# Short convolution and spatial gating: transposes off TensorE, tap products on ScalarE

## The chip, the cores and the metric

The kernel runs on one core of a Trainium2 chip (trn2). The metric is the time of one execution in device microseconds (us); each kernel is run several times and the median is given. The profile is taken from one execution of its own, whose span runs from the first to the last instruction of the core.

## The reference

A trunk of four layers works on x, 256 tokens by 1024 channels, in float32. Each layer is

```
x = x + 0.5 * swiglu(rms_norm(x), gate, up, down)      # D_FF = 2816
x = x + mixer(rms_norm(x))
x = x + 0.5 * swiglu(rms_norm(x), gate, up, down)
```

and the mixer is the short gated convolution in layers 0 and 3, latent attention in layer 1, and the spatial-gating MLP in layer 2. The two that matter here:

```
def short_conv_mixer(x, w_in, conv_k, w_out):
    b, c, h = split(x @ w_in, 3)               # 1024 channels each
    z = c * h
    conv[t] = k[0]*z[t-2] + k[1]*z[t-1] + k[2]*z[t]     # per channel, causal
    return (b * conv) @ w_out

def spatial_gating_mixer(x, w_in, v_norm, w_s, b_s, w_out):
    u, v = split(gelu(x @ w_in), 2)
    mixed = causal w_s over chunks of 128 tokens of rms_norm(v) + b_s
    return (u * mixed) @ w_out
```

## The kernel before, in words

**Tiles and products.** The tokens are two tiles of 128, each worked on by a stream of its own (stream 0 and stream 1, a Python generator each). Every product x @ w is done in split float32: weights and activations are each cut into a high part (fp32r) and a low part, and `products` (L293 to L302) issues three matmuls per 128 rows of weights and 512 columns: high by high (L299), high by low (L300), low by high (L302). The activations are the stationary operand, so they have to stand with channels on the partitions. The weights come in units of 128 x 1024 values: SyncE loads `raw` (L93), ScalarE makes `whi` (L106), VectorE makes `wlo` (L113). Six raw buffers and nine buffers for made units; a unit is made four units ahead of stream 0 (`AHEAD`).

**Order.** Nothing is reordered by a scheduler: the order of the program is the order on each engine's queue, and each queue is worked off in order. `advance(t)` lets one stream go on to its next yield, which is as a rule one unit: six matmuls of 512 columns. One such advance is called a turn here. Stream 0 gets four turns ahead, then the streams alternate, stream 1 first; so stream 1 does the same step seven turns after stream 0. Weights are made in stream 0's turns.

**Work that is put off.** `later(n, fn)` puts a piece of work off by a number of turns; `run_due` issues what is due at the end of each turn, in order of due turn and then of registration. The counter is raised between the stream's step and `run_due`, so a piece put off by n from a stream's step in turn a is issued at the end of turn a+n-1; put off from another put-off piece, at the end of the n-th turn after it.

**The convolution block** of a stream, in steps of one unit each: before the change the steps 1 to 12 are a group of three products, c0, h0 and b0 (halves of 512 columns; done at steps 8, 10, 12), then c1 (13 to 16), h1 (17 to 20), b1 (21 to 24). Steps 25 to 32 are the product with w_out in `rows_into_x`: steps 25 to 28 take channels of half 0 (`ms[0]`), 29 and 30 those of half 1 (`ms[1]`) for output columns 0 to 511, 31 and 32 for columns 512 to 1023. `c_done` copies its bank to SBUF on ScalarE (L544), `h_done` multiplies on VectorE (L548) to z, `b_done` copies on ScalarE (L553). `convolved` turns z with four PE transposes (L261 in `transposed`), copies them on ScalarE to zT (L523, 128 x 512), and makes the convolution on VectorE: four 128 x 128 products (L528) and eight multiply-adds (L530). `gated` turns b with four PE transposes, multiplies on VectorE (L537), and `split` makes the high part on ScalarE (L253) and the low part on VectorE (L254).

**Two ways to turn.** x itself is turned at the block ends either by PE (`turn_by_pe`) or, in `prepare_x`, by a 32 x 32 block transpose on VectorE (L415), a write of 256 KB to DRAM (L421) and four reads of 64 KB (L425) on SyncE's queue, and four 128 x 128 activations on ScalarE that scale while they copy (L431, `take`, 12 turns after). Weight loads are held back (`W.hold`) from the write until the reads are issued. `turned` does the same for the feed-forward's hidden values.

**The spatial block.** `u_mixed` (L639) multiplies, `gated` turns with PE and splits (`lhs_of`), for both halves, two turns later.

Of the kernel before, what the change touches and what calls it, by code (L numbers as in the profile page):

```python
# [48 lines left out]
CHAIN_AHEAD = 3  # L49
LAG = 4  # L50
DOWN_TAIL, OUT_TAIL = 12, 4
X_TURN, X_WRITE, X_READ, X_TAKE = 2, 1, 3, 12
IDLE_FIRST, IDLE_DMA, IDLE_PE, IDLE_MLA = 1, 2, 2, 4
SKEW = 2
K_POOL, K_SUM, K_SCALE, K_TURN, Q_ROPE, Q_TURN, Q_SUM, Q_WAIT = 2, 2, 3, 2, 1, 3, 3, 3
# [76 lines left out]
def trunk(ctx: ExitStack, tc: tile.TileContext, x, positions, norm_g, ffn_gate, ffn_up, ffn_down,  # L132
# [76 lines left out]
    def column(at, n=1):  # L209
        return columns[1][:, at : at + n]  # L210
# [39 lines left out]
    def split(src, shape):  # L250

        hi, lo = slot(shape, F32R), slot(shape, F32R)
        nc.scalar.activation(hi, src, AF.Copy)  # L253
        nc.vector.tensor_tensor(out=lo, in0=src, in1=hi.bitcast(F32), op=ALU.subtract)  # L254
        return hi, lo

    def transposed(parts):

        tr = trp()
        for n, part in enumerate(parts):  # L260
            nc.tensor.transpose(tr[: part.shape[-1], n, :], part, ident)  # L261
        return tr
# [129 lines left out]
    def x_half(t, h):  # L392
        return xs[t][:, h * 512 : (h + 1) * 512]
# [12 lines left out]
    def prepare_x(t, h, i, which, halves_by_dma):  # L406

        g = gain_at(i, which, h)
        lhs[t][h] = None
        later(1, lambda: square_x(t, h))  # L410
        if not halves_by_dma[h]:
            later(X_TURN, lambda: turn_by_pe(t, h, g))
            return
        z = slot([P, 4, 4, 32])
        nc.vector.transpose(z.rearrange("p j k b -> p k j b"), x_half(t, h).rearrange("p (k j b) -> p k j b", j=4, b=32))  # L415
        d = dram.tile([4, 32, 4, 4, 32], F32, tag="xturn", name=name("xturn"))
        y = slot([P, 4, 4, 32])

        def write():
            W.hold(1)  # L420
            nc.sync.dma_start(out=d.rearrange("i a j k b -> (i a) j k b"), in_=z)  # L421

        def read():
            for j in range(4):
                nc.sync.dma_start(out=y[32 * j : 32 * j + 32], in_=d[:, :, j].rearrange("i a k b -> a i k b"))  # L425
            W.hold(-1)

        def take():
            xg = slot([P, 4, P])
            for k in range(4):  # L430
                nc.scalar.activation(xg[:, k, :].rearrange("p (i b) -> p i b", b=32), y[:, :, k], AF.Copy, scale=g[:, k : k + 1])  # L431
            lhs[t][h] = split(xg, [P, 4, P])

        later(X_WRITE, write)
        later(X_READ, read)
        later(X_TAKE, take)

    def turn_by_pe(t, h, g):
        tr = transposed([xs[t][:, (4 * h + k) * P : (4 * h + k + 1) * P] for k in range(4)])
# [64 lines left out]


    def plan_conv(ia):
        plan_group([(conv_w_in[ia], part * D) for part in (1, 2, 0)], 512, NK)
        for part in (1, 2, 0):
            W.add(conv_w_in[ia], part * D + 512, 512, NK, 2)
        plan_rows(conv_w_out[ia], NK, OUT_TAIL)  # L510

    def conv(t, i, ia, shared, then):
        a, r = yield from normed(t, IDLE_DMA)
        ms = [None] * 2

        def convolved(j, z):
            zp = transposed([z[:, k * P : (k + 1) * P] for k in range(4)])
            zT = slot([P, 4, P + 2])
            if t == 0:
                nc.vector.memset(zT[:, :, 0:2], 0.0)  # L520
            else:
                nc.vector.tensor_copy(out=zT[:, :, 0:2], in_=shared["z", t - 1, j][:, :, P : P + 2])
            nc.scalar.activation(zT[:, :, 2 : P + 2], zp, AF.Copy)  # L523
            shared["z", t, j] = zT
            cv = slot([P, 4, P])
            for k in range(4):
                taps = [column(C_CONV + (3 * ia + w) * NK + 4 * j + k) for w in range(3)]
                nc.vector.tensor_scalar(cv[:, k, :], zT[:, k, 0:P], taps[0], None, op0=ALU.mult)  # L528
                for w in (1, 2):
                    nc.vector.scalar_tensor_tensor(out=cv[:, k, :], in0=zT[:, k, w : w + P], scalar=taps[w],  # L530
                                                   in1=cv[:, k, :], op0=ALU.mult, op1=ALU.add)
            shared["cv", t, j] = cv

        def gated(j, bs):
            bT = transposed([bs[:, k * P : (k + 1) * P] for k in range(4)])
            m = slot([P, 4, P])
            nc.vector.tensor_tensor(out=m, in0=bT, in1=shared["cv", t, j], op=ALU.mult)  # L537
            ms[j] = split(m, [P, 4, P])

        cs = [None] * 2  # L540

        def c_done(j, ps):
            cs[j] = slot([P, 512])
            nc.scalar.activation(cs[j], ps, AF.Copy, scale=r)  # L544

        def h_done(j, ps):
            z = slot([P, 512])
            nc.vector.scalar_tensor_tensor(out=z, in0=ps, scalar=r, in1=cs[j], op0=ALU.mult, op1=ALU.mult)  # L548
            later(3, lambda: convolved(j, z))

        def b_done(j, ps):
            bs = slot([P, 512])
            nc.scalar.activation(bs, ps, AF.Copy, scale=r)  # L553
            later(2, lambda: gated(j, bs))

        yield from linear_group(t, a, 512, NK, [lambda ps, f=f: f(0, ps) for f in (c_done, h_done, b_done)])
        for f in (c_done, h_done, b_done):
            f(1, (yield from linear(t, a, 512, NK)))
            yield
        yield from rows_into_x(t, lambda k: ms[k // 4], NK, OUT_TAIL, 1.0, then)  # L560

# [31 lines left out]
    def spatial(t, i, ic, _, then):  # L593
# [30 lines left out]
                                    in1=column(C_SGB + 4 * j, 4).unsqueeze(2).broadcast_to([P, 4, P]))  # L624
            mixed[j] = mx

        def gated(j, m):
            ms[j] = lhs_of(m, 4)

        us = [None] * 2  # L630

# [5 lines left out]
        def u_mixed(j):  # L637
            m = slot([P, 512])
            nc.vector.tensor_tensor(out=m, in0=us[j], in1=mixed[j].rearrange("p k n -> p (k n)"), op=ALU.mult)  # L639
            later(2, lambda: gated(j, m))  # L640

        yield from linear_group(t, a, 512, NK, [v_done, v_done, lambda ps: u_done(0, ps)])
        u_done(1, (yield from linear(t, a, 512, NK)))
# [392 lines left out]
```

## Time and profile before

| | |
|---|---|
| median of 3 runs | 1859.11 us (1858.88 to 1860.58) |
| the profiled execution | 1856.6 us |
| its span | 1854.9 us, mean granted TensorE clock 0.998 |
| PE busy | 1833.3 us, 99% of the span |
| VectorE (DVE) busy | 1119.6 us, 60% |
| ScalarE (ACT) busy | 913.9 us, 49% |
| GpSimd (POOL) busy | 103.9 us, 6% |
| DMA | mean 216 GB/s, 400.26 MB |

Busy time is the time in which an engine had at least one instruction in work; waits and instruction issue don't count. On PE the instructions overlap, so the distance from one start to the next tells what one costs. In a timeline a row is one or more like instructions in a row; the bracket tells how long the engine stood idle before it and what released it. The clock of 1 means 2.4 GHz, 0.5 means 1.2 GHz.

### The profile page before, as it was taken

How to read it: one execution, taken by the hardware profiler on the slowest of the kernel's cores; microseconds unless marked ns; L12 is line 12 of the kernel's file. 1: busy time of each engine (PE TensorE's matmuls, PEld its weight loads, DVE VectorE, ACT ScalarE, POOL GpSimd, SP SyncE). 2: the span in 40 equal slices, each digit the busy share in tenths (PEclk: the TensorE clock that was granted, in tenths of full speed). 3: DMA queues.
4: the chain of work that ended last, by engine and by line, in shares of the span. 5: the costliest groups of instructions: out<-in, count | busy, mean ns of one | idle time of the engine just before them, and what ended most of it. 6: DMA issues, size and time to landing. Idle time of an engine off the chain costs nothing.

```text
span 1854.9 us, 23375 instructions
## 1 busy us (share of the span) xinstructions
PE 1833.3 (99%) x8518; PEld 1506.0 (81%) x8518; DVE 1119.6 (60%) x1357; ACT 913.9 (49%) x1300; POOL 103.9 (6%) x222
## 2 busy tenths in 40 slices
PE   8999999999999989999999999999999999999999
PEld 6888878888888878888888888888888888788887
DVE  5655676655665576666556555665645665775662
ACT  5443645443644376544454446554545454545451
POOL 1000000000501031000010001000000000000000
PEclk9999999999999999999999999999999999999999
DMA  7776657776777550687777766577857785657782
GB/s 265 241 240 218 209 179 216 240 241 210 235 244 238 193 160 15 201 259 232 221 238 256 228 220 216 175 232 234 264 185 243 242 261 178 213 181 235 233 269 75
DMA packets 228980, 400.26 MB, mean 216 GB/s; under 512 B 17126, under 2 KB 77696, under 8 KB 228864
## 3 DMA queue, kind: packets, MB, share of 16 engines
q1 hardware_dynamic: 227856, 397.08, 67.0%
q8 instruction: 66, 1.08, 0.2%
q0 software_dynamic: 608, 1.11, 0.2%
q10 hardware_dynamic: 400, 0.57, 0.1%
q14 instruction: 50, 0.41, 0.1%
HBM read 365.67 MB, written 33.03 MB: 215 GB/s over the span
## 4 chain that ended last, share of the span: by engine, by line
PE 96%; ACT 2%; DVE 2%; issue 0%; DMA 0%; DVEq 0%; ACTq 0%
PE acc L299 31%; PE acc L300 31%; PE acc L302 31%; PE tr L261 1%; PE acc L938 1%; PE acc L911 1%; ACT whi L106 1%; DVE wlo L113 0%; DVE s L530 0%; ACT s L836 0%; ACT s L253 0%; PE acc L620 0%; DMA s<-in_norm_g_dram 0%; ACT s L817 0%; ACT s L860 0%
## 5 line engine op out<-in xcount | busy, mean ns | idle before, releaser
L299 PE MATMUL acc<-whi,s 128*128 128x512 f32 (+1 forms) x2664 | 1025.2, 385 | 2.8 <-ACT whi L106 1.3
L300 PE MATMUL acc<-wlo,s 128*128 128x512 f32 (+1 forms) x2664 | 1019.8, 383 | 2.1 <-DVE wlo L113 2.1
L302 PE MATMUL acc<-whi,s 128*128 128x512 f32 (+1 forms) x2664 | 988.2, 383 | 0.0
L113 DVE TENSOR_TENSOR wlo<-raw,whi 128x1024 fp32r<-128x1024 f32 (+1 forms) x634 | 747.3, 1212 | 131.0 <-ACT whi L106 129.2
L106 ACT ACTIVATE whi<-raw 128x1024 fp32r<-128x1024 f32 (+1 forms) x634 | 636.6, 1047 | 138.9 <-PE acc L302 120.3
L299 PEld LDWEIGHTS acc<-whi,s 128*128 128x128 f32 x2664 | 500.9, 188 | 107.8 <-ACT whi L106 2.5
L300 PEld LDWEIGHTS acc<-wlo,s 128*128 128x128 f32 x2664 | 501.0, 188 | 106.0 <-DVE wlo L113 3.0
L302 PEld LDWEIGHTS acc<-whi,s 128*128 128x128 f32 x2664 | 500.7, 188 | 106.1 <-DVE s L254 0.7
L479 ACT ACTIVATE s<-acc,rstd 128x512 f32<-128x512 f32 (+1 forms) x96 | 62.6, 652 | 446.4 <-PE acc L302 440.4
L487 DVE SCALAR_TENSOR_TENSOR s<-acc,rstd,s 128x512 f32<-128x512 f32 (+1 forms) x96 | 67.7, 705 | 173.6 <-PE acc L302 171.8
L286 DVE TENSOR_TENSOR s<-big,s 128x512 fp32r<-128x512 f32 x96 | 61.8, 644 | 128.1 <-ACT s L285 127.9
L381 ACT ACTIVATE s<-x 128x512 bf16<-128x512 f32 x48 | 30.2, 630 | 163.6 <-DVE x L400 125.9
L254 DVE TENSOR_TENSOR s<-s,s 128x512 fp32r<-128x512 f32 (+1 forms) x58 | 39.9, 688 | 107.6 <-ACT s L253 107.6
L389 POOL TENSOR_TENSOR total<-ss,ss 128x1 f32<-128x1 f32 x26 | 14.8, 570 | 1417.1 <-ACT s L381 1417.1
L400 DVE SCALAR_TENSOR_TENSOR x<-acc,x 128x512 f32<-128x512 f32 x32 | 22.1, 692 | 117.3 <-PE acc L302 117.2
L285 ACT ACTIVATE s<-big 128x512 fp32r<-128x512 f32 x96 | 56.3, 586 | 22.1 <-DMA big<-turn 22.0
L489 DVE STREAM_TRANSPOSE big<-s 128x512 f32<-128x512 f32 (+1 forms) x96 | 64.1, 667 | 3.3
L253 ACT ACTIVATE s<-s 128x512 fp32r<-128x512 f32 (+1 forms) x58 | 36.5, 629 | 42.1 <-DVE s L537 21.6
L431 ACT ACTIVATE s<-s,columns 128x128 f32<-128x128 f32 x136 | 43.1, 388 | 1.9 <-DMA s<-xturn 1.7
L261 PE MATMUL tr<-ident,s 128*128 128x128 f32 (+1 forms) x222 | 33.3, 276 | 9.8 <-DVE s L781 5.1
L261 PEld LDWEIGHTS tr<-ident,s 128*128 128x128 f32 (+1 forms) x222 | 25.8, 138 | 17.9 <-DVE s L781 7.3
L415 DVE STREAM_TRANSPOSE s<-x 128x512 f32<-128x512 f32 x34 | 24.2, 711 | 1.2
(123 smaller groups left out, 410.6 us busy)
## 6 DMA issues: line engine op xcount, KB each, us to landing
raw<-in_ffn_gate_dram SPq DMA_DIRECT2D x176, 512.0 KB, 4.8
raw<-in_ffn_up_dram SPq DMA_DIRECT2D x176, 512.0 KB, 5.0
raw<-in_ffn_down_dram SPq DMA_DIRECT2D x176, 512.0 KB, 5.0
raw<-in_conv_w_in_dram SPq DMA_DIRECT2D x48, 512.0 KB, 4.7
turn<-big SPq DMA_DIRECT2D x32, 512.0 KB, 4.0
big<-turn SPq DMA_DIRECT2D x128, 128.0 KB, 4.4
xturn<-s SPq DMA_DIRECT2D x34, 256.0 KB, 4.2
s<-xturn SPq DMA_DIRECT2D x136, 64.0 KB, 2.0
```

The lines of the kernel that those rows point to most:

```text
L106: nc.scalar.activation(hi, src, AF.Copy)
L113: self.nc.vector.tensor_tensor(out=lo, in0=src, in1=hi.bitcast(F32), op=ALU.subtract)
L261: nc.tensor.transpose(tr[: part.shape[-1], n, :], part, ident)
L285: nc.scalar.activation(hi.rearrange("p k (i b) -> p k i b", b=32), src, AF.Copy)
L286: nc.vector.tensor_tensor(out=lo.rearrange("p k (i b) -> p k i b", b=32), in0=src, in1=hi.bitcast(F32).rearrange("p k (i b) -> p k i b", b ...
L299: nc.tensor.matmul(ps, lhsT=ah[:, k, :], rhs=wh[:, wk, c], start=first, stop=False)
L300: nc.tensor.matmul(ps, lhsT=ah[:, k, :], rhs=wl[:, wk, c], start=False, stop=False)
L302: nc.tensor.matmul(ps, lhsT=al[:, k, :], rhs=wh[:, wk, c], start=False, stop=last)
L431: nc.scalar.activation(xg[:, k, :].rearrange("p (i b) -> p i b", b=32), y[:, :, k], AF.Copy, scale=g[:, k : k + 1])
L479: nc.scalar.activation(sg[n], ps[:, :w], AF.Silu, scale=r)
L487: nc.vector.scalar_tensor_tensor(out=h, in0=ps[:, :w], scalar=r, in1=sg[n], op0=ALU.mult, op1=ALU.mult)
L489: nc.vector.transpose(z[0][:, :, k0 : k0 + w // P].rearrange("p j k b -> p k j b"), h.rearrange("p (k j b) -> p k j b", j=4, b=32))
```

## The change

z and b in the convolution, and the second half of the gate in the spatial block, are turned in the way that x is: VectorE block transpose, DMA to DRAM and back. The function `turn_half` is cut out of `prepare_x` for it. The tap products go from VectorE to ScalarE: four copies of 128 x 128 into zT, twelve activations of 128 x 128 with the tap as scale, one tile per tap; VectorE adds the three tiles one turn later. The two columns ahead of zT are filled by GpSimd. The products of the block are done in another order: the group is c0, h0, c1 (done at steps 8, 10, 12), then h1 (16), b0 (20), b1 (24). `Z_TAKE` and `M_TAKE` are both 9.

```diff
-X_TURN, X_WRITE, X_READ, X_TAKE = 2, 1, 3, 12
+X_TURN, X_WRITE, X_READ, X_TAKE, Z_TAKE, M_TAKE = 2, 1, 3, 12, 9, 9
...
+    def turn_half(src, take, turns):
+
         z = slot([P, 4, 4, 32])
-        nc.vector.transpose(z.rearrange("p j k b -> p k j b"), x_half(t, h).rearrange("p (k j b) -> p k j b", j=4, b=32))
-        d = dram.tile([4, 32, 4, 4, 32], F32, tag="xturn", name=name("xturn"))
+        nc.vector.transpose(z.rearrange("p j k b -> p k j b"), src.rearrange("p (k j b) -> p k j b", j=4, b=32))
+        d = dram.tile([4, 32, 4, 4, 32], F32, tag="xturn", name=name("xturn"), bufs=8)
         y = slot([P, 4, 4, 32])
 
         def write():
...
         later(X_WRITE, write)
         later(X_READ, read)
-        later(X_TAKE, take)
+        later(turns, lambda: take(y))
...
-        plan_group([(conv_w_in[ia], part * D) for part in (1, 2, 0)], 512, NK)
-        for part in (1, 2, 0):
-            W.add(conv_w_in[ia], part * D + 512, 512, NK, 2)
+        w = conv_w_in[ia]
+        plan_group([(w, D), (w, 2 * D), (w, D + 512)], 512, NK)
+        for c in (2 * D + 512, 0, 512):
+            W.add(w, c, 512, NK, 2)
...
-        def convolved(j, z):
-            zp = transposed([z[:, k * P : (k + 1) * P] for k in range(4)])
+        def convolved(j, y):
             zT = slot([P, 4, P + 2])
             if t == 0:
-                nc.vector.memset(zT[:, :, 0:2], 0.0)
+                nc.gpsimd.memset(zT[:, :, 0:2], 0.0)
             else:
-                nc.vector.tensor_copy(out=zT[:, :, 0:2], in_=shared["z", t - 1, j][:, :, P : P + 2])
-            nc.scalar.activation(zT[:, :, 2 : P + 2], zp, AF.Copy)
+                nc.gpsimd.tensor_copy(out=zT[:, :, 0:2], in_=shared["z", t - 1, j][:, :, P : P + 2])
+            for k in range(4):
+                nc.scalar.activation(zT[:, k, 2 : P + 2].rearrange("p (i b) -> p i b", b=32), y[:, :, k], AF.Copy)
             shared["z", t, j] = zT
-            cv = slot([P, 4, P])
-            for k in range(4):
-                taps = [column(C_CONV + (3 * ia + w) * NK + 4 * j + k) for w in range(3)]
-                nc.vector.tensor_scalar(cv[:, k, :], zT[:, k, 0:P], taps[0], None, op0=ALU.mult)
-                for w in (1, 2):
-                    nc.vector.scalar_tensor_tensor(out=cv[:, k, :], in0=zT[:, k, w : w + P], scalar=taps[w],
-                                                   in1=cv[:, k, :], op0=ALU.mult, op1=ALU.add)
+            cv = [slot([P, 4, P]) for _ in range(3)]
+            for w in range(3):
+                for k in range(4):
+                    nc.scalar.activation(cv[w][:, k, :], zT[:, k, w : w + P], AF.Copy, scale=column(C_CONV + (3 * ia + w) * NK + 4 * j + k))
+            later(1, lambda: summed(j, cv))
+
+        def summed(j, parts):
+            cv = parts[0]
+            for part in parts[1:]:
+                nc.vector.tensor_tensor(out=cv, in0=cv, in1=part, op=ALU.add)
             shared["cv", t, j] = cv
 
-        def gated(j, bs):
-            bT = transposed([bs[:, k * P : (k + 1) * P] for k in range(4)])
+        def gated(j, y):
             m = slot([P, 4, P])
-            nc.vector.tensor_tensor(out=m, in0=bT, in1=shared["cv", t, j], op=ALU.mult)
+            nc.vector.tensor_tensor(out=m.rearrange("p k (i b) -> p i k b", b=32), in0=y,
+                                    in1=shared["cv", t, j].rearrange("p k (i b) -> p i k b", b=32), op=ALU.mult)
             ms[j] = split(m, [P, 4, P])
...
-            later(3, lambda: convolved(j, z))
+            turn_half(z, lambda y: convolved(j, y), Z_TAKE)
...
-            later(2, lambda: gated(j, bs))
-
-        yield from linear_group(t, a, 512, NK, [lambda ps, f=f: f(0, ps) for f in (c_done, h_done, b_done)])
-        for f in (c_done, h_done, b_done):
-            f(1, (yield from linear(t, a, 512, NK)))
+            turn_half(bs, lambda y: gated(j, y), M_TAKE)
+
+        yield from linear_group(t, a, 512, NK, [lambda ps: c_done(0, ps), lambda ps: h_done(0, ps), lambda ps: c_done(1, ps)])
+        for f, j in ((h_done, 1), (b_done, 0), (b_done, 1)):
+            f(j, (yield from linear(t, a, 512, NK)))
             yield
...
-        def gated(j, m):
-            ms[j] = lhs_of(m, 4)
+        def gated(j, y):
+            src = y.rearrange("p i k b -> p k i b")
+            hi, lo = slot([P, 4, P], F32R), slot([P, 4, P], F32R)
+            nc.scalar.activation(hi.rearrange("p k (i b) -> p k i b", b=32), src, AF.Copy)
+            nc.vector.tensor_tensor(out=lo.rearrange("p k (i b) -> p k i b", b=32), in0=src,
+                                    in1=hi.bitcast(F32).rearrange("p k (i b) -> p k i b", b=32), op=ALU.subtract)
+            ms[j] = hi, lo
...
-            later(2, lambda: gated(j, m))
+            if j == 0:
+                later(2, lambda: gated_by_pe(j, m))
+            else:
+                turn_half(m, lambda y: gated(j, y), M_TAKE)
```

## Rows read from the trace of the kernel before

**Rows 1.** Page, busy time of each engine, share of the span, instructions.

```profile
PE 1833.3 (99%) x8518; PEld 1506.0 (81%) x8518; DVE 1119.6 (60%) x1357; ACT 913.9 (49%) x1300; POOL 103.9 (6%) x222
```

**Rows 2.** Page, the chain that ended last, by engine and by line.

```profile
PE 96%; ACT 2%; DVE 2%; issue 0%; DMA 0%; DVEq 0%; ACTq 0%
```

**Rows 3.** Timeline, PE: one turn of six matmuls; start us, duration us.

```profile
204.64 0.39 PE L302 MATMUL acc<-whi,s 128*128 128x512 f32 x1
...
206.03 0.39 PE L302 MATMUL acc<-whi,s 128*128 128x512 f32 x1
```

**Rows 4.** Timeline, first convolution, stream 0: h0 done, then its transposes.

```profile
218.60 0.39 PE L302 MATMUL acc<-whi,s 128*128 128x512 f32 x1
218.83 0.39 PE L299 MATMUL acc<-whi,s 128*128 128x512 f32 x1
...
219.11 0.75 DVE L548 SCALAR_TENSOR_TENSOR s<-acc,rstd,s 128x512 f32<-128x512 f32 x1
...
221.38 0.39 PE L302 MATMUL acc<-whi,s 128*128 128x512 f32 x1
221.61 0.60 PE L261 MATMUL tr<-ident,s 128*128 128x128 f32 x4
221.97 0.48 PE L299 MATMUL acc<-whi,s 128*128 128x512 f32 x1
...
222.28 0.40 PE L300 MATMUL acc<-wlo,s 128*128 128x512 f32 x1
```

**Rows 5.** Timeline, PE, second convolution, stream 1: transposes that came late.

```profile
1607.76 0.40 PE L302 MATMUL acc<-whi,s 128*128 128x512 f32 x1
1609.09 0.66 PE L261 MATMUL tr<-ident,s 128*128 128x128 f32 x4 [0.93 <-DVE s L548]
```

**Rows 6.** Timeline, ScalarE: a bank copied, then the next instruction.

```profile
223.22 0.39 PE L302 MATMUL acc<-whi,s 128*128 128x512 f32 x1
...
223.45 0.40 PE L299 MATMUL acc<-whi,s 128*128 128x512 f32 x1
...
223.71 0.69 ACT L544 ACTIVATE s<-acc,rstd 128x512 f32<-128x512 f32 x1 [0.86 <-PE acc L302]
...
224.29 1.05 ACT L106 ACTIVATE whi<-raw 128x1024 fp32r<-128x1024 f32 x1
```

**Rows 7.** Timeline, ScalarE: four scaled copies, and three weight units.

```profile
187.46 1.26 ACT L431 ACTIVATE s<-s,columns 128x128 f32<-128x128 f32 x4
...
215.91 2.94 ACT L106 ACTIVATE whi<-raw 128x1024 fp32r<-128x1024 f32 x3
```

**Rows 8.** Groups by line and form: count, busy us, mean ns, idle before.

```profile
L113 DVE TENSOR_TENSOR wlo<-raw,whi 128x1024 fp32r<-128x1024 f32 x626 | 739.7, 1215 | 129.5 <-ACT whi L106 128.6 <-DMA raw<-in_ffn_up_dram 0.5 <-DMA turn<-big 0.3
L431 ACT ACTIVATE s<-s,columns 128x128 f32<-128x128 f32 x136 | 43.1, 388 | 1.9 <-DMA s<-xturn 1.7
L254 DVE TENSOR_TENSOR s<-s,s 128x512 fp32r<-128x512 f32 x56 | 38.8, 693 | 106.4 <-ACT s L253 106.4
L253 ACT ACTIVATE s<-s 128x512 fp32r<-128x512 f32 x56 | 35.4, 632 | 38.6 <-DVE s L537 21.6 <-DVE s L441 15.9
L415 DVE STREAM_TRANSPOSE s<-x 128x512 f32<-128x512 f32 x34 | 24.2, 711 | 1.2
L530 DVE SCALAR_TENSOR_TENSOR s<-s,columns,s 128x128 f32<-128x128 f32 x64 | 22.5, 352 | 2.3
L398 DVE TENSOR_TENSOR x<-acc,x 128x512 f32<-128x512 f32 x16 | 11.0, 690 | 9.1 <-PE acc L302 9.1
L528 DVE TENSOR_SCALAR s<-s,columns 128x128 f32<-128x128 f32 x32 | 9.0, 283 | 9.8 <-ACT s L523 9.8
L639 DVE TENSOR_TENSOR s<-s,s 128x512 f32<-128x512 f32 x4 | 2.8, 689 | 2.8 <-ACT s L634 2.8
L634 ACT ACTIVATE s<-acc,rstd 128x512 f32<-128x512 f32 x4 | 2.7, 681 | 4.6 <-PE acc L302 4.6
```

**Rows 9.** What ScalarE waited for: us in total, times, longest us.

```profile
ACT whi L106 <- PE acc L302: 120.3, 82, 1.8
```

**Rows 10.** DMA issues by line: count, KB each, median us to landing.

```profile
xturn<-s SPq DMA_DIRECT2D x34, 256.0 KB, 4.2
s<-xturn SPq DMA_DIRECT2D x136, 64.0 KB, 2.0
```

**Rows 11.** One line's instructions (L421, the write): time from issue to landing.

```profile
DMA to landing us min/median/max: 2.0/4.2/6.6
```

**Rows 12.** Timeline, SyncE: the four reads of one turned half.

```profile
178.03 1.75 SPq L425 DMA_DIRECT2D s<-xturn  x4
```

**Rows 13.** Timeline, PE, attention block: matmuls after two waits.

```profile
678.47 0.79 PE L299 MATMUL acc<-whi,s 128*128 128x512 f32 x1 [1.31 <-ACT s L253]
...
681.19 0.38 PE L300 MATMUL acc<-wlo,s 128*128 128x384 f32 x1
```

**Rows 14.** Windows: us, busy by engine, granted clock, DMA share, GB/s.

```profile
676.00:678.00 2.00, 0.64 (x4) 0.39 (x4) 1.86 (x5) 1.05 (x3) 1.12 (x1) 0.97 0.59 236
678.00:680.00 2.00, 1.53 (x4) 1.25 (x5) 1.49 (x7) 1.97 (x9) 1.01 (x3) 0.50 0.64 183
```

More of the change, by code (lines that the diff above doesn't have):

```diff
@@ L413, in prepare_x, with take @@
             return
+        def take(y):
+            xg = slot([P, 4, P])
+            for k in range(4):
+                nc.scalar.activation(xg[:, k, :].rearrange("p (i b) -> p i b", b=32), y[:, :, k], AF.Copy, scale=g[:, k : k + 1])
+            lhs[t][h] = split(xg, [P, 4, P])
+        turn_half(x_half(t, h), take, X_TAKE)
+    def turn_half(src, take, turns):
         z = slot([P, 4, 4, 32])
-        nc.vector.transpose(z.rearrange("p j k b -> p k j b"), x_half(t, h).rearrange("p (k j b) -> p k j b", j=4, b=32))
-        d = dram.tile([4, 32, 4, 4, 32], F32, tag="xturn", name=name("xturn"))
+        nc.vector.transpose(z.rearrange("p j k b -> p k j b"), src.rearrange("p (k j b) -> p k j b", j=4, b=32))
+        d = dram.tile([4, 32, 4, 4, 32], F32, tag="xturn", name=name("xturn"), bufs=8)
         y = slot([P, 4, 4, 32])
@@ L426, in read @@
             W.hold(-1)
-        def take():
-            xg = slot([P, 4, P])
-            for k in range(4):
-                nc.scalar.activation(xg[:, k, :].rearrange("p (i b) -> p i b", b=32), y[:, :, k], AF.Copy, scale=g[:, k : k + 1])
-            lhs[t][h] = split(xg, [P, 4, P])
         later(X_WRITE, write)
         later(X_READ, read)
-        later(X_TAKE, take)
+        later(turns, lambda: take(y))
     def turn_by_pe(t, h, g):
@@ L514, in conv @@
         ms = [None] * 2
-        def convolved(j, z):
-            zp = transposed([z[:, k * P : (k + 1) * P] for k in range(4)])
+        def convolved(j, y):
             zT = slot([P, 4, P + 2])
             if t == 0:
-                nc.vector.memset(zT[:, :, 0:2], 0.0)
+                nc.gpsimd.memset(zT[:, :, 0:2], 0.0)
             else:
-                nc.vector.tensor_copy(out=zT[:, :, 0:2], in_=shared["z", t - 1, j][:, :, P : P + 2])
-            nc.scalar.activation(zT[:, :, 2 : P + 2], zp, AF.Copy)
+                nc.gpsimd.tensor_copy(out=zT[:, :, 0:2], in_=shared["z", t - 1, j][:, :, P : P + 2])
+            for k in range(4):
+                nc.scalar.activation(zT[:, k, 2 : P + 2].rearrange("p (i b) -> p i b", b=32), y[:, :, k], AF.Copy)
             shared["z", t, j] = zT
-            cv = slot([P, 4, P])
-            for k in range(4):
-                taps = [column(C_CONV + (3 * ia + w) * NK + 4 * j + k) for w in range(3)]
-                nc.vector.tensor_scalar(cv[:, k, :], zT[:, k, 0:P], taps[0], None, op0=ALU.mult)
-                for w in (1, 2):
-                    nc.vector.scalar_tensor_tensor(out=cv[:, k, :], in0=zT[:, k, w : w + P], scalar=taps[w],
-                                                   in1=cv[:, k, :], op0=ALU.mult, op1=ALU.add)
+            cv = [slot([P, 4, P]) for _ in range(3)]
+            for w in range(3):
+                for k in range(4):
+                    nc.scalar.activation(cv[w][:, k, :], zT[:, k, w : w + P], AF.Copy, scale=column(C_CONV + (3 * ia + w) * NK + 4 * j + k))
[4 more added lines that the diff above has]
+                nc.vector.tensor_tensor(out=cv, in0=cv, in1=part, op=ALU.add)
             shared["cv", t, j] = cv
-        def gated(j, bs):
-            bT = transposed([bs[:, k * P : (k + 1) * P] for k in range(4)])
+        def gated(j, y):
             m = slot([P, 4, P])
-            nc.vector.tensor_tensor(out=m, in0=bT, in1=shared["cv", t, j], op=ALU.mult)
+            nc.vector.tensor_tensor(out=m.rearrange("p k (i b) -> p i k b", b=32), in0=y,
+                                    in1=shared["cv", t, j].rearrange("p k (i b) -> p i k b", b=32), op=ALU.mult)
             ms[j] = split(m, [P, 4, P])
@@ L639, in u_mixed, with gated_by_pe @@
             nc.vector.tensor_tensor(out=m, in0=us[j], in1=mixed[j].rearrange("p k n -> p (k n)"), op=ALU.mult)
-            later(2, lambda: gated(j, m))
+            if j == 0:
+                later(2, lambda: gated_by_pe(j, m))
+            else:
+                turn_half(m, lambda y: gated(j, y), M_TAKE)
+        def gated_by_pe(j, m):
+            ms[j] = lhs_of(m, 4)
         yield from linear_group(t, a, 512, NK, [v_done, v_done, lambda ps: u_done(0, ps)])
```

## The prediction

> **What bounds the kernel now.** The page comes first: PE is busy 99% of the span, VectorE 60%, ScalarE 49% [rows 1]. The chain that ended last is PE for 96% [rows 2]. So a matmul taken away is time gained, and every wait of PE is time lost, one for one. ScalarE's mean says nothing of one moment: what counts is what stands in its queue when PE needs something. Then the timelines. A turn of six matmuls lasts 206.03 - 204.64 = 1.39 us [rows 3]. In the convolution, h0 of stream 0 is done when the next turn starts at 218.83; its transposes, put off by 3, start at 221.61, which is 2.78 us or two turns later [rows 4]. So a piece put off by n runs n-1 whole turns after the end of the turn that asked for it, as the code reads; by this I place the new pieces. ScalarE runs a little ahead of PE, but not freely: its weight units wait 120.3 us in all for PE to free a buffer, 1.8 us at most [rows 9], and a copy out of a bank waits for PE by its nature [rows 6].
>
> **What the change removes.** Two convolutions x two streams x two halves x two values are 16 sets of four transposes, the spatial block's second half 2 more: 18. One set: from the L302 at 221.38, the second matmul after it would start 0.46 later and starts at 222.28, 0.90 later [rows 4]. That is 0.44 a set, 7.9 us in all. Also gone is a wait for z in stream 1, once a block: the transposes start at 1609.09 and not 0.23 after 1607.76, so 1.1 us late [rows 5]; 2.2 us for both blocks. Removed: **10.1 us**.
>
> **What it costs the other engines.** VectorE loses 32 products and 64 multiply-adds (9.0 + 22.5 us), and gains 18 block transposes of 0.71 and 16 additions, taken at the 0.69 of a 128 x 512 operation [rows 8]: some 8 us less. ScalarE gains 8 bursts of 16 activations. The nearest row is L431, the same 128 x 128 scaled copy: 0.388 us alone, but four in 1.26, so (1.26 - 0.388)/3 = 0.29 from start to start [rows 7, 8]. Sixteen: 4.64 us. The four without a scale may be cheaper; I know no row for them and keep 0.29. At 0.2 each for all (a lower end, an estimate: half of 0.388) a burst is 3.2 us, at 0.388 end to end 6.2 us. I take 4.64, since L431 is the same operation. GpSimd's two columns are needed first by the fifth of the 16, and GpSimd is idle (103.9 us of the span, rows 1): no cost; without this cover it would be some tenths.
>
> The Trainium skill ("ScalarE: Activation LUTs", Rules for kernel authors) budgets about 0.3 us for an activation plus 0.83 ns an element. That is 0.41 us for 128 elements, 6.5 us a burst; the sum below would rise by 2 x 1.9 us, to about 1876 us. The row shows 0.29 from start to start, so the trace does not bear the budget out for activations in a row.
>
> **Where the bursts stand.** Call the turn in which stream 0 finishes b0 turn 0. Stream 1 does the same step at turn 7. Stream 1 finishes h1 four steps, eight turns, earlier, at turn -1; its take is put off by 9, so it is issued at the end of turn 7, just behind the copy of stream 1's own b0, which waits for PE to finish turn 7. Stream 0 finishes b1 at turn 8; at the end of turn 8 its take for b0 is issued (m, high part, low part), and PE needs the high part at turn 10. ScalarE's queue is then: copy of stream 1's b0; 16 activations; the unit of turn 8; copy of stream 0's b1; high part. On VectorE the block transpose of b1 stands ahead of m. From the end of turn 7: 0.26 until the copy starts (223.71 after the turn's end at 223.45) and 0.58 until the next instruction starts [rows 6]; 4.64 for the burst; 0.95 for the unit ((2.94 - 1.05)/2, rows 6, 7); 0.69 copy of b1 [rows 6]; 0.71 transpose; 0.69 m; 0.63 high part [rows 8]. Sum 9.15 us. PE has turns 8 and 9 to do, 2.78 us. It waits **6.4 us**, in each of two blocks: 12.8. At the two ends for the burst: 5.0 and 8.0 us a block.
>
> The other takes wait as well, by the same handovers. Stream 1's first: the copy of its b1 ends turn 15, its take comes at the end of turn 15, and it is needed at turn 17: 0.26 + 0.69 + 0.71 + 0.69 + 0.63 = 2.98 against one turn, so 1.6 us. Stream 0's second half (end of turn 16, needed at 18) queues behind that one's low part: 0.69 + 0.69 + 0.63 = 2.01 against 1.39, so 0.6 us. Stream 1's second half (end of turn 23, needed at 25) has no bank copy before it: nothing, at worst 0.4. Per block 2.2, both **4.4 us**.
>
> **The clock.** After PE's waits around 676 to 678 us the granted clock is 0.50, that is 1.2 GHz [rows 14], and from 678.47 to 681.19 the matmuls run at half speed [rows 13]: half of 2.72, about 1.4 us lost. A wait of 6.4 us is longer than that one, so I add 1.4 a block, **2.8 us**; the lower end is 0.
>
> **The spatial block.** Its take is registered from a put-off piece, so it comes a turn later, directly ahead of its use. Stream 0: 0.26 + 0.68 (gate) + 0.69 + 0.71 + 1.22 (wlo) + 0.69 (low part) = 4.25 after the turn, against two turns and the two matmuls that go without the low part, 3.24: 1.0 us. Stream 1: its low part queues behind stream 0's last residual and its block transpose: 0.26 + 0.69 + 0.71 + 0.69 = 2.35 against 0.46: 1.9 us [rows 6, 8]. Together **2.9 us**; the lower end is 0.
>
> **Transfers.** A turned half lands 0.26 + 0.75 (L548, rows 4) + 0.71 + 4.2 (write) + 1.75 (issue of four reads) + 2.0 = 9.7 us after the turn's end [rows 8, 10, 12]; the take is due after 8 turns, 11.1 us. Hidden by 1.4 us. SyncE issues the write and the reads in order ahead of the held weight loads; six raw buffers and four made units are more than ten turns of cover, so PE does not see it. Without that cover each half would delay a load by the 4.2 us of its write. The new order of products moves no work: as many units, the same bytes.
>
> **Sum.** Added 12.8 + 4.4 + 2.8 + 2.9 = 22.9, removed 10.1: **12.8 us slower**. The profiled execution took 1856.6 us for a span of 1854.9; it becomes 1869.4. The median shown is 2.5 us above that execution, so I forecast 1859.1 + 12.8 = 1871.9, say **1872 us**. With all lower ends (burst 3.2, no clock, no spatial wait) added is 10.0 + 4.4 = 14.4, so 1863.4; with the upper burst 26.1, so 1875.1. The likeliest case's own range is 1863 to 1877.
>
> **Rivals.**
> *ScalarE gets its burst done ahead of the bank copy; faster.* If the takes came one turn earlier than I count, the burst of stream 1 would stand ahead of its b0 copy, and m ahead of b1's transpose. The values land 9.7 us or seven turns after turn -1, at the start of turn 7; from there 4.64 + 0.58 + 0.63 = 5.9 against three turns, 4.2: 1.7 us a block is all that stays. 10.1 - 3.4 = 6.7 gained: 1852.4 us. It is decided by that one turn. For it: ScalarE is idle half of the span. Against it: the two turns read at 221.61 [rows 4]. 0.2, which takes in that ScalarE's order is otherwise kinder than I read it.
> *The burst is cheap and the late turns hide in slack.* Waits of about 10 us in all: within 0.2%, 1859. It needs a burst below 3.2 us and no wait in the other takes. 0.1.
> *A turned half comes late.* If a write takes the 6.6 us of the longest one before [rows 11], a half lands after 12.1 us and the take waits 1 us at the head of ScalarE's queue, and what is behind it too; some 2 us a block, 1876. For it: the two writes of turns 7 and 8 queue on SyncE, the second behind a late copy. 0.1.
> *Transposes were not the bound.* If PE's time moved elsewhere the change would give nothing; the 0.44 us on PE between matmuls speak against it. It is within the second rival.
> The forecast: 0.6.
>
> **Chances and range.** Measurements of this kernel tell 0.2%, 3.7 us, from no change. Faster 0.2, within 0.1, slower 0.7. The range holds the forecast, the rival in its place and the late transfers: 1851 to 1878.
>
> **What would show it.** Right: in both convolutions one PE wait of about 6 us before an L299, released by ScalarE's high part in `split`; ahead of it on ScalarE 16 activations in a row, then whi, a copy, the high part; about 0.50 of clock after it; two smaller waits six to eight turns later. PE instructions 8518 - 72 = 8446; ScalarE busy some 36 us more (128 activations at 43.1/136, less eight copies). Wrong: PE as dense in the convolutions as before, or the burst ahead of the bank copy; a PE wait released by VectorE's multiply with ScalarE idle would mean that the transfer was late.

## The result and the profile after

| | median, us | runs |
|---|---|---|
| before | 1858.99 | 1857.05 to 1860.58, 4 runs |
| after | 1883.05 | 1881.91 to 1885.57, 4 runs |
| ratio | 1.0133 | 95% interval 1.0117 to 1.0149 |

The change makes the kernel 24.1 us slower, about twice the 12.8 us of the forecast and outside the range. The page's busy row and the chain of the kernel after, against [rows 1, 2]:

```profile
PE 1836.4 (97%) x8446; PEld 1503.9 (80%) x8446; DVE 1112.6 (59%) x1287; ACT 943.4 (50%) x1420; POOL 105.0 (6%) x230
...
PE 91%; DMA 3%; ACT 3%; DVE 2%; issue 1%; SPq 0%; DVEq 0%; ACTq 0%
```

PE has the 72 instructions fewer that were forecast, and its busy time is 3 us longer all the same: matmuls at half clock are longer. The span of this execution is 1883.9 us (before: 1854.9), and the chain now runs through a DMA and through ScalarE. The view of waits says where PE stood (us in all, times, longest us):

```profile
PE acc L299 <- ACT s L253: 24.9, 9, 10.1
...
PE acc L302 <- DVE s L640: 2.4, 2, 1.6
```

Before, the first of these rows was one wait of 1.3 us and the second did not exist. Cutting both traces at the start of stream 1's last residual of each block gives the stages. The four rows that differ, and all others within 1.3 us:

| stage, us | before | after | difference |
|---|---|---|---|
| first convolution | 94.79 | 105.30 | +10.5 |
| attention block | 105.66 | 108.63 | +3.0 |
| spatial block | 73.24 | 75.29 | +2.1 |
| second convolution | 94.68 | 106.94 | +12.3 |

The three blocks that the diff touches add 24.8 us, the whole of the median's 24.1. The attention block's 3.0 us are not taken as the change's: with the same code of this block, it took 105.5 to 105.8 us in five of the experiments below, 107.0 to 107.7 in three and 108.6 in two. The mean granted clock in it was 0.968 before and 0.937 in this execution. This execution is the longest of the four of after.

PE's timeline in the first convolution, from the turn before stream 0's gate, and the long wait of the second (start us, duration us; in brackets the time idle before it and what ended that):

```profile
260.30 0.40 PE L302 MATMUL acc<-whi,s 128*128 128x512 f32 x1
269.12 0.80 PE L299 MATMUL acc<-whi,s 128*128 128x512 f32 x1 [8.43 <-ACT s L253]
...
274.84 0.46 PE L300 MATMUL acc<-wlo,s 128*128 128x512 f32 x1
...
283.17 0.50 PE L299 MATMUL acc<-whi,s 128*128 128x512 f32 x1 [1.37 <-ACT s L253]
...
285.16 0.50 PE L299 MATMUL acc<-whi,s 128*128 128x512 f32 x1 [0.34 <-ACT s L253]
...
296.67 0.50 PE L299 MATMUL acc<-whi,s 128*128 128x512 f32 x1 [0.80 <-ACT s L253]
...
1651.43 0.40 PE L302 MATMUL acc<-whi,s 128*128 128x512 f32 x1
1661.97 0.80 PE L299 MATMUL acc<-whi,s 128*128 128x512 f32 x1 [10.15 <-ACT s L253]
```

Matmuls follow each other by 0.23 us at full clock, so the first gap costs 269.12 - 260.30 - 0.23 = 8.59 us. In the second convolution it is 1661.97 - 1651.43 - 0.23 = 10.31. Three smaller gaps follow, 1.53, 0.49 and 0.96 us by the same reckoning, alike in both blocks. ScalarE's timeline of the long wait, with the head of the second block's burst in the last row, against [rows 6, 7]:

```profile
257.94 0.69 ACT L562 ACTIVATE s<-acc,rstd 128x512 f32<-128x512 f32 x1 [1.30 <-PE acc L302]
261.09 0.91 ACT L529 ACTIVATE s<-s 128x128 f32<-128x128 f32 x4 [2.46 <-DMA s<-xturn]
261.90 3.60 ACT L534 ACTIVATE s<-s,columns 128x128 f32<-128x128 f32 x12
265.41 1.04 ACT L106 ACTIVATE whi<-raw 128x1024 fp32r<-128x1024 f32 x1
266.35 0.67 ACT L562 ACTIVATE s<-acc,rstd 128x512 f32<-128x512 f32 x1
268.44 0.63 ACT L253 ACTIVATE s<-s 128x512 fp32r<-128x512 f32 x1 [1.42 <-DVE s L545]
...
1653.94 0.91 ACT L529 ACTIVATE s<-s 128x128 f32<-128x128 f32 x4 [4.20 <-DMA s<-xturn]
```

This is the queue of the prediction, entry by entry: copy of stream 1's b0, 16 activations, one unit, copy of stream 0's b1, then the high part for which PE waits. One thing is new: the burst stands still for 2.46 us (4.20 in the second convolution) at its head until the turned half has landed. SyncE's timeline and the landing of the two writes issued at 250.1 and 250.7 say why, against [rows 10, 11]:

```profile
245.93 1.75 SPq L436 DMA_DIRECT2D s<-xturn  x4
247.78 1.80 SPq L93 DMA_DIRECT2D raw<-in_conv_w_out_dram  x4
250.10 0.93 SPq L432 DMA_DIRECT2D xturn<-s  x2
```

```profile
DMA to landing us min/median/max: 7.6/7.6/7.6
```

Four weight loads of 512 KB, held back until the earlier reads were out, leave together just ahead of the two writes. The writes then take 7.6 us to land (8.3 and 8.4 in the second convolution), not the median of 4.2. Windows of after around the wait (window, its length, busy us of PE, PEld, DVE, ACT and POOL, granted clock, DMA share, GB/s), against [rows 14]:

```profile
264.00:267.00 3.00, 0.00 (x0) 0.00 (x0) 0.00 (x0) 3.00 (x8) 0.00 (x0) 0.62 0.94 328
267.00:270.00 3.00, 0.88 (x2) 0.78 (x3) 2.18 (x4) 1.58 (x4) 0.00 (x0) 0.50 0.94 329
270.00:273.00 3.00, 3.00 (x8) 2.33 (x8) 2.96 (x4) 1.91 (x3) 0.00 (x0) 0.50 0.41 151
273.00:276.00 3.00, 3.00 (x10) 2.34 (x10) 2.67 (x3) 0.00 (x0) 0.00 (x0) 0.67 0.50 137
```

PE has nothing to do in the first of these windows; the granted clock is 0.62 in it and 0.50, 1.2 GHz, in the next two, though PE is busy all through the third. From 269.12 to 274.84 the matmuls start 0.43 us apart instead of 0.23.

### The profile page after: what moved, and what is told of

Read it like the earlier page. It is cut to its first block, busy times and chain, and to the rows that moved or that the text cites. A ratio compares the mean times of both kernels' runs of the same rounds, so it can differ in the third digit from the quotient of the medians.

```text
span 1883.9 us, 23468 instructions
## 1 busy us (share of the span) xinstructions
PE 1836.4 (97%) x8446; PEld 1503.9 (80%) x8446; DVE 1112.6 (59%) x1287; ACT 943.4 (50%) x1420; POOL 105.0 (6%) x230
## 4 chain that ended last, share of the span: by engine, by line
PE 91%; DMA 3%; ACT 3%; DVE 2%; issue 1%; SPq 0%; DVEq 0%; ACTq 0%
PE acc L299 29%; PE acc L302 29%; PE acc L300 29%; DMA xturn<-s 2%; PE tr L261 1%; ACT whi L106 1%; DVE wlo L113 1%; PE acc L958 1%; DMA s<-xturn 1%; PE acc L931 1%; ACT s L534 1%; DMA raw<-in_ffn_gate_dram 0%; SPq L436 0%; ACT s L253 0%; DMA raw<-in_conv_w_out_dram 0%
## 5 line engine op out<-in xcount | busy, mean ns | idle before, releaser
L261 PE MATMUL tr<-ident,s 128*128 128x128 f32 (+1 forms) x150 | 24.5, 294 | 8.1 <-DVE s L801 5.2
L426 DVE STREAM_TRANSPOSE s<-s 128x512 f32<-128x512 f32 x18 | 12.6, 707 | 28.5 <-ACT s L562 28.1
L261 PEld LDWEIGHTS tr<-ident,s 128*128 128x128 f32 (+1 forms) x150 | 18.3, 143 | 13.8 <-DVE s L801 7.2
```

## The experiments

Two theories stood: the bursts of 16 activations stand in ScalarE's queue ahead of what PE needs (the prediction's), or the turned halves come late. Each kernel below is timed against the kernel before on the same chip; that kernel's median was 1858.5 to 1858.7 us in all of these batches.

**The bursts two turns later.**

```diff
-X_TURN, X_WRITE, X_READ, X_TAKE, Z_TAKE, M_TAKE = 2, 1, 3, 12, 9, 9
+X_TURN, X_WRITE, X_READ, X_TAKE, Z_TAKE, M_TAKE = 2, 1, 3, 12, 11, 9
```

> Z_TAKE 11 in place of 9, nothing else: the 16 activations of stream 1's second half of z are issued at the end of turn 9, behind the high part that PE waits for. Theory (the burst's place in ScalarE's queue plus a late landing of the gate): the long wait of PE shrinks from 8.6 and 10.3 us to what the landing of stream 0's gate alone sets, 3 to 6 us a block, and the kernel is 8 to 12 us faster than the changed one, 1871 to 1876 us. Rival (only the late transfers count, whatever stands in the queue): the waits stay near 8 to 10 us and the time at 1883. Rival (ScalarE as a whole has too much to do): no change either.

Measured: 1874.37 us, ratio 1.0082 (1.0062 to 1.0102); the long waits are 4.98 and 4.71 us. ScalarE's timeline:

```profile
264.01 0.63 ACT L253 ACTIVATE s<-s 128x512 fp32r<-128x512 f32 x1 [4.83 <-DVE s L545]
264.55 0.89 ACT L529 ACTIVATE s<-s 128x128 f32<-128x128 f32 x4
```

The burst now follows the high part, and ScalarE is idle for 4.83 us ahead of it: m itself is late. VectorE's row for m says why:

```profile
263.29 0.69 DVE L545 TENSOR_TENSOR s<-s,s 128x512 f32<-128x512 f32 x1 [3.36 <-DMA s<-xturn]
```

So the place of the burst carries part of the wait, and with the burst out of the way the transfer still holds PE.

**No hold of the weight loads around these writes.** Only x's writes hold them.

```diff
-    def turn_half(src, take, turns):
+    def turn_half(src, take, turns, held=False):
...
-            W.hold(1)
+            if held:
+                W.hold(1)
...
-            W.hold(-1)
+            if held:
+                W.hold(-1)
```

> The changed kernel, but weight loads are not held back while a half of z, of the gate or of the spatial product is on its way (for x they are, as before). Theory (held loads leave together, four of 512 KB just ahead of the next writes, which then take 7.6 us): the writes land 2 to 4 us sooner, ScalarE's waits for the landing (2.5 and 4.2 us ahead of the deciding bursts) go to 0 to 1, the long waits of PE fall to about 6 us, the place in the queue alone, and the time to 1874 to 1879 us. Rival (the write is slow because the chip's queues are busy with weights anyway): landing and time unchanged.

Measured: 1877.40 us, ratio 1.0098 (1.0078 to 1.0118). The two writes, and ScalarE's and PE's timelines:

```profile
DMA to landing us min/median/max: 4.3/4.7/5.0
```

```profile
259.08 0.69 ACT L564 ACTIVATE s<-acc,rstd 128x512 f32<-128x512 f32 x1 [1.89 <-PE acc L302]
259.66 0.90 ACT L531 ACTIVATE s<-s 128x128 f32<-128x128 f32 x4
...
267.68 0.80 PE L299 MATMUL acc<-whi,s 128*128 128x512 f32 x1 [5.86 <-ACT s L253]
```

The same writes land after 4.3 to 5.0 us, and the burst starts as soon as the copy ahead of it ends. What is left of the long wait is 5.86 us in one block and 5.87 in the other: this is the price of the queue place alone, forecast at 6.4. The 2.6 and 4.3 us above it (8.43 and 10.15 less these) are the late landing. The two writes still stand behind three loads, but these were issued 1.1 us apart, the four of the changed kernel 0.5 us apart. Where loads come close together without a hold, the write is late all the same: issued at 260.54 behind three loads 0.5 us apart, it takes 7.65 us in this run.

**The taps back on VectorE**, after the four copies on ScalarE.

```diff
-            cv = [slot([P, 4, P]) for _ in range(3)]
-            for w in range(3):
-                for k in range(4):
-                    nc.scalar.activation(cv[w][:, k, :], zT[:, k, w : w + P], AF.Copy, scale=column(C_CONV + (3 * ia + w) * NK + 4 * j + k))
-            later(1, lambda: summed(j, cv))
...
+            cv = slot([P, 4, P])
+            for k in range(4):
+                taps = [column(C_CONV + (3 * ia + w) * NK + 4 * j + k) for w in range(3)]
+                nc.vector.tensor_scalar(cv[:, k, :], zT[:, k, 0:P], taps[0], None, op0=ALU.mult)
+                for w in (1, 2):
+                    nc.vector.scalar_tensor_tensor(out=cv[:, k, :], in0=zT[:, k, w : w + P], scalar=taps[w],
+                                                   in1=cv[:, k, :], op0=ALU.mult, op1=ALU.add)
```

> The tap products are VectorE's again (four products, eight multiply-adds, directly after ScalarE's four copies); everything else as in the changed kernel. Theory (what counts is that a half's convolution stands ahead of the deciding m, on whichever engine): the twelve VectorE operations of 0.33 us stand ahead of b1's transpose and m, the long waits are 7 to 8 us in the first block and 9 to 10 in the second, and the time 1879 to 1883 us. Rival (moving the taps to ScalarE is the fault): the long waits go and the time is under 1865 us.

Measured: 1881.72 us, ratio 1.0121 (1.0101 to 1.0142); long waits 7.28 and 6.67 us. ScalarE's copies, then VectorE's timeline:

```profile
262.65 0.91 ACT L529 ACTIVATE s<-s 128x128 f32<-128x128 f32 x4 [3.04 <-DMA s<-xturn]
...
263.06 0.29 DVE L534 TENSOR_SCALAR s<-s,columns 128x128 f32<-128x128 f32 x1 [2.72 <-ACT s L529]
...
266.95 0.71 DVE L426 STREAM_TRANSPOSE s<-s 128x512 f32<-128x512 f32 x1
```

The twelve products now stand on VectorE ahead of b1's block transpose, and PE still waits. The time and the first wait are as expected; the second was expected at 9 to 10 us. In both waits a landing is contained, 3.04 and 2.43 us at the head of ScalarE's copies. Less these, 4.24 us are left in each block, against 5.97 and 5.95 in the changed kernel (8.43 less 2.46, 10.15 less 4.20). So the taps hold PE from either engine when they run directly ahead of something PE needs, from VectorE for some 1.7 us less.

**Both causes taken away, and the gate a turn earlier.** The edit of the second experiment, with `Z_TAKE` 11 and `M_TAKE` 8.

> Z_TAKE 11, M_TAKE 8 and no hold for these halves. Theory: with the burst behind the high part, m ahead of the next bank's block transpose, and the gate landing in time, all of PE's waits in the three blocks go but for 0 to 2 us each; what is left is the 10 us saved, 1849 to 1856 us, faster than before. Rival (the way over DRAM is too slow for eight turns): waits for the landing of 2 to 5 us stay in each block, released by VectorE's m with ScalarE idle, and the time is 1858 to 1870 us.

Measured: 1862.83 us, ratio 1.0020 (1.0010 to 1.0029): the theory missed. The time is the rival's, but only the first of the waits that stay is one for the landing, and they are shorter than its 2 to 5 us. VectorE's timeline and PE's, and a window behind the second wait:

```profile
270.58 0.69 DVE L547 TENSOR_TENSOR s<-s,s 128x512 f32<-128x512 f32 x1 [0.73 <-DMA s<-xturn]
...
272.58 1.22 DVE L113 TENSOR_TENSOR wlo<-raw,whi 128x1024 fp32r<-128x1024 f32 x1
273.71 0.70 DVE L426 STREAM_TRANSPOSE s<-s 128x512 f32<-128x512 f32 x1
274.34 0.65 DVE L547 TENSOR_TENSOR s<-s,s 128x512 f32<-128x512 f32 x1
```

```profile
271.99 0.50 PE L299 MATMUL acc<-whi,s 128*128 128x512 f32 x1 [1.24 <-ACT s L253]
...
275.71 0.50 PE L299 MATMUL acc<-whi,s 128*128 128x512 f32 x1 [2.05 <-ACT s L253]
...
277.00:280.00 3.00, 3.00 (x8) 2.33 (x8) 1.99 (x2) 1.49 (x2) 0.00 (x0) 0.50 0.61 175
```

Some 20 us of the 24 are gone, of them 2.5 in the spatial block (72.80 us), whose waits no longer appear. In each convolution two waits stay, 1.24 and 2.05 us (0.33 and 1.22, then 2.06, in the second). At the first, m waits for its landing: with `M_TAKE` 8 there is a turn less of cover. At the second, m stands behind a weight unit and a block transpose. That is the gate's own path. Behind this second wait the granted clock is 0.50 with PE busy, in both convolutions. No run shows what the gate's earlier turn gave by itself.

**The same with these writes on GpSimd's queue.**

```diff
-            nc.sync.dma_start(out=d.rearrange("i a j k b -> (i a) j k b"), in_=z)
+            (nc.sync if held else nc.gpsimd).dma_start(out=d.rearrange("i a j k b -> (i a) j k b"), in_=z)
```

> The kernel with Z_TAKE 11, M_TAKE 8 and no hold, and the writes of these halves to DRAM on GpSimd's queue; the reads stay on SyncE's. Theory (a write on SyncE's queue lands late because it stands behind weight loads of the same queue, up to 7.4 us before): it lands in 2 to 4.5 us, the gate's halves are there 2 to 3 us sooner, the two waits left in each convolution (1.4 and 2.2 us) fall under 0.5 us, the clock stays at 1, and the time is 1849 to 1856 us. Rival (all queues share the same DMA engines, so the write is as slow from any queue): writes of 4 to 7 us as before, 1860 to 1865 us.

Measured: 1859.38 us, ratio 1.0008 (0.9999 to 1.0017). The writes of the first convolution land after 3.6, 5.2 and 7.5 us (least, median, most), against 4.3, 4.5 and 7.4 from SyncE; so a queue of its own makes no write faster. The Trainium skill ("DMA: Bandwidth & Descriptors", Issuing engines are not separate DMA queues) says that transfers started by different engines interleave on the same 16 DMA engines; the landing times agree. A new wait shows on ScalarE:

```profile
265.07 1.28 ACT L536 ACTIVATE s<-s,columns 128x128 f32<-128x128 f32 x4 [1.14 <-POOL s L529]
```

GpSimd's copy of the two columns stood behind a write that was waiting for its data. Of the 3.5 us between this run and the one above, the three stages of the two profiles show 1.5 (95.39, 72.37 and 96.62 against 96.43, 72.80 and 96.64). Of these, 1.0 lie in the first convolution, where PE still waits 0.44, 0.97 and 2.05 us but the granted clock stays at 1 this time. The attention block, which neither edit touches, differs by 1.9; where the rest lies is not settled.

**The new order of products alone**, in the kernel before: `plan_conv` and the last lines of `conv` as in the change, everything else as before.

> The kernel before with the convolution's products in the new order (c0, h0, c1, then h1, b0, b1), PE transposes and VectorE taps kept. Theory (the order moves no work and puts nothing new in front of PE): within 0.2% of before, 1856 to 1861 us; the wait of 1.1 us for z in stream 1 may go, 2 us less. Rival (the order is part of the loss): over 1865 us, with waits of PE for the gate, since b1 is now the last product ahead of w_out.

Measured: 1856.92 us, ratio 0.9991 (0.9981 to 1.0000). Each convolution is 1.0 to 1.2 us shorter (93.61 and 93.67): the wait for z [rows 5] is gone. The gain comes from the order, and it needs no DMA; the median itself is at the edge of the noise.

**z alone over DRAM.** The change with `Z_TAKE` 11 and without the hold, but the two gates turned by PE:

```diff
-        def gated(j, y):
+        def gated(j, bs):
+            bT = transposed([bs[:, k * P : (k + 1) * P] for k in range(4)])
...
-            turn_half(bs, lambda y: gated(j, y), M_TAKE)
+            later(2, lambda: gated(j, bs))
...
-            if j == 0:
-                later(2, lambda: gated_by_pe(j, m))
-            else:
-                turn_half(m, lambda y: gated(j, y), M_TAKE)
+            later(2, lambda: gated_by_pe(j, m))
```

> Only z goes over DRAM (Z_TAKE 11, no hold, ScalarE taps, new order); the gate and the spatial block are turned by PE as before. Theory (the loss is in the gate's way, which has eight turns to its use, while z has over twenty): PE saves 8 sets of 0.44 and two waits of 1.1 us, 5.7 us, with no new wait over 0.5 us: 1852 to 1856 us, faster than before. Rival (a late z holds ScalarE's queue wherever it is): PE waits of 2 us or more in the convolutions, 1858 to 1866 us.

Measured: 1854.02 us, ratio 0.9977 (0.9968 to 0.9986): faster than both kernels. The convolutions take 92.02 and 92.01 us, that is 2.7 less than before; the order's 1.1 and four sets of 0.44 make 2.9. The window of the first one in which the changed kernel waited longest:

```profile
255.00:270.00 15.00, 15.00 (x70) 12.17 (x69) 9.14 (x12) 14.70 (x36) 0.00 (x0) 1.00 0.51 159
```

ScalarE is busy 14.70 us of 15 here, with all taps on it, and PE never stops. So a full ScalarE costs nothing here, where nothing with a due time stands behind the burst.

**The taps alone on ScalarE**, in the kernel before, with PE's transposes and the old order (the activations and `summed` as in the change).

> The kernel before with the tap products on ScalarE and the additions on VectorE, one turn later; transposes by PE, old order, so this part of the change alone. Theory (twelve activations of 0.29 us in ScalarE's queue cost nothing where nothing that PE needs stands behind them): VectorE has 3.9 us less ahead of stream 1's z, the two waits of 1.1 us go, 1855 to 1860 us. Rival (the burst on ScalarE is the cost by itself): PE waits of 2 us or more released by ScalarE, 1862 us or over.

Measured: 1868.95 us, ratio 1.0059 (1.0044 to 1.0074): the theory missed again, the rival held. ScalarE's timeline, and PE's wait:

```profile
226.13 3.62 ACT L528 ACTIVATE s<-s,columns 128x128 f32<-128x128 f32 x12
...
231.17 0.67 ACT L556 ACTIVATE s<-acc,rstd 128x512 f32<-128x512 f32 x1
...
231.89 0.66 PE L261 MATMUL tr<-ident,s 128*128 128x128 f32 x4 [2.25 <-ACT s L556]
```

The expectation had overlooked the copy of b (L556), which PE's transposes need two turns later. With twelve activations ahead of it PE waits 2.25 and 1.70 us in the first convolution, 2.25 and 1.67 in the second.

**z alone, with the bursts at their old turn:** the kernel of 1854.02 us with `Z_TAKE` 9 in place of 11.

> The faster kernel (only z over DRAM, gate by PE) with Z_TAKE 9 in place of 11: the burst of stream 1's second half of z stands again at the end of turn 7, now ahead of the copy of stream 0's b1 that PE's transposes need at the end of turn 9. Theory (place in ScalarE's queue): 0.26 + 0.58 + 4.32 + 0.95 + 0.69 = 6.8 us from the end of turn 7 against two turns, 2.8: a wait of 4.0 us in each convolution, some more of landing and 1.5 to 3 us of clock, so 10 to 14 us slower than with 11: 1863 to 1868 us. Rival (the gate's way over DRAM made all of the loss, z's place nothing): 1852 to 1856 us, as with 11.

Measured: 1864.56 us, ratio 1.0031 (1.0021 to 1.0041), 10.5 us more than with 11. The timelines of ScalarE and PE:

```profile
258.38 0.90 ACT L531 ACTIVATE s<-s 128x128 f32<-128x128 f32 x4
...
263.63 0.67 ACT L564 ACTIVATE s<-acc,rstd 128x512 f32<-128x512 f32 x1
...
264.36 1.11 PE L261 MATMUL tr<-ident,s 128*128 128x128 f32 x4 [3.37 <-ACT s L564]
```

One constant, no other work: the 16 activations ahead of the copy of b1 cost 3.37 us of wait, where 4.0 were expected, and 4.8 to 4.9 us a block. This shows the queue's place by itself: the burst starts without a wait for a DMA.

**z and the spatial half over DRAM:** the same kernel with `Z_TAKE` 11, the spatial block's second half as in the change and `M_TAKE` 8.

> The faster kernel with the second half of the spatial gate over DRAM as well, put off by 8 turns. Theory: one turn earlier than in the changed kernel takes its low part out from behind the residual and the unit, so the waits of 0.9 and 1.8 us go and the two sets of 0.44 stay saved: 0.4 to 0.9 us less, 1852 to 1854 us. Rival (the extra transfers cost as much as they save): 1854 to 1856 us.

Measured: 1853.90 us, ratio 0.9975 (0.9965 to 0.9985). The spatial block takes 72.46 us, 0.76 less than with PE's transposes; the median cannot be told from 1854.02. This kernel and the one of 1862.83 us differ in the convolution's gate alone, so its way over DRAM costs 8.9 us, with the bursts out of its way and no hold.

## Why the prediction was right in direction and wrong in size

| term, us | forecast | measured |
|---|---|---|
| removed: 18 sets of transposes, two waits for z | -10.1 | 2 x 1.1 + 16 x 0.41 + 0.8 = -9.5 |
| long waits, two | +12.8 | 8.59 + 10.31 = +18.9 |
| later takes of both blocks | +4.4 | 2 x (1.53 + 0.49 + 0.96) = +6.0 |
| half clock after the long waits | +2.8 | 2.8 + 2.7 = +5.5 |
| matmuls 0.34 to 0.39 us apart behind each smaller wait | 0 | 2 x 0.85 = +1.7 |
| spatial block | +2.9 | +2.7 |
| sum | +12.8 | +25.3 |

The stages add up to 24.8, the medians differ by 24.1; together the terms are 0.5 to 1.2 us too large.

*Removed.* Held: 1.1 us a block by the order alone, and 1.63 by the four sets of z (92.0 against 93.64), 0.41 a set where 0.44 was forecast. b's sets are taken as equal to z's, and were not taken away by themselves; the spatial block's two gave 0.76.

*Where the bursts stand.* Held: the order of ScalarE's queue, the turn, and the size without the landing, 5.9 against 6.4. The burst was a little cheaper than its row: copies without a scale start (0.91 - 0.298)/3 = 0.20 us apart, the taps (3.60 - 0.387)/11 = 0.29, in all 4.3 us in place of 4.64; ScalarE's busy time rose by 29.5 us where 36 were forecast. Here 0.298 and 0.387 are the mean of one activation of each line.

*Transfers.* **This step failed.** It said "Hidden by 1.4 us", with the write at its median of 4.2 us. The writes took 7.6 us in the first convolution and 8.3 to 8.4 in the second, and the values came 2.46 and 4.20 us after ScalarE was ready for them. Taking the hold away took the landing to 4.3 to 5.0 us, and ScalarE's wait for it went. The text named the hold, and then looked only at whether PE would run out of weights, not at what the held loads do when they are let go: they leave together, right ahead of the next write. It looked up the whole spread (2.0 to 6.6), gave the longest to a rival with a chance of 0.1 and priced that at 2 us a block; the cost was 2.6 and 4.3, and it came in both blocks. Its sign of a late transfer, a wait ended by VectorE's multiply with ScalarE idle, was not the one to look for: the lateness stood at the head of the burst (L529).

*The later takes.* Stream 1's first was forecast at 1.6 and measured 1.53, stream 0's second 0.6 and 0.49; stream 1's second was taken as nothing, "at worst 0.4", and is 0.96. VectorE's timeline has what that sum left out, a weight unit directly ahead of m; no run tries it by itself:

```profile
294.07 1.22 DVE L113 TENSOR_TENSOR wlo<-raw,whi 128x1024 fp32r<-128x1024 f32 x1 [0.26 <-ACT whi L106]
295.21 0.68 DVE L545 TENSOR_TENSOR s<-s,s 128x512 f32<-128x512 f32 x1
```

*The clock.* **The size was off, by a factor of two.** The mechanism was there. The model was a wait of 1.3 us with 2.7 us at half clock behind it; after 8.4 and 10.2 us of idleness the half clock lasts 5.7 and 5.5 us. How long it lasts did not follow the length of the wait: in the second experiment waits of 5.86 and 5.87 us have 6.0 and 3.6 us of it behind them. So that the price came out at twice the row's is in part chance. Nor was the row the price of one wait of 1.3 us: PE was busy for only 0.64 of the 2 us from 676 to 678 [rows 14], and the waits of 1.37 us in the changed kernel are followed at full clock. The prediction said that its wait was longer than the row's and then took the row's price.

*The spatial block.* Held: 0.88 and 1.80 us of gaps against 1.0 and 1.9, ended by VectorE's low part (L640), as worked out.

*The rivals.* "ScalarE gets its burst done ahead of the bank copy" fell: the turn was counted rightly. "The burst is cheap" fell. "A turned half comes late" came true, on top of the forecast's queue as its 1876 us had it; it had 0.1. What lay between 1876 and 1883 is the rest of its price, with the clock's and that of the smaller waits. "Transposes were not the bound" fell with the run of z alone, in which fewer of them gave time back.

What the faster versions show is that the idea had a gain in it. z has slack, since its use waits for b; the gate has none. z alone, at a turn where nothing waits behind its taps, gives 0.23% (0.14 to 0.32), about what the order and z's four sets a block are worth.

## What to carry to other kernels

Work that is put off in an in-order queue is placed by what stands behind it: look up which entry of the same engine PE needs next, and issue the burst after that entry, for one constant was worth 10.5 us here with the same work. Move a value to a longer path only where its use has slack to spare: with the bursts well placed, z and the spatial half gave 1853.9 us, and with the convolution's gate as well 1862.8. When transfers are held back for a small one, look at what the held ones do when they are let go, and price a landing by the moment it falls in, not by the median of a quiet one.

## What was not expected of the hardware

- The half clock, 1.2 GHz, stayed for 3.6 to 6.2 us after restarts from waits of 4.7 to 10.2 us, with PE busy throughout, and not in the order of the waits. After waits of 3.37 and 3.38 us it stayed for 3.2 and 2.8.
- After shorter waits the same code gave both: behind waits of 2.05 us the clock fell to half in three blocks and stayed at 1 in one (the first of the run with GpSimd's writes); behind 2.25 us, in the run with the taps alone, it fell in the second block and not in the first.
- A 256 KB write landed after 7.6 to 8.4 us when four loads of 512 KB had been issued 0.5 us apart just ahead of it, after 7.7 and 7.9 behind three 0.5 us apart, and after 4.3 to 5.0 behind three 1.1 us apart.
- Activations of 128 x 128 in a row start 0.20 us apart without a scale by column and 0.29 with one, though one alone takes 0.30 and 0.39.
